# Huber loss on one core: a block of 32x2560 numbers taken apart from the tiles, with a full second tile and narrower end tiles

## The chip, the cores and the metric

The kernel runs on one core of one Trainium2 chip. The metric is the time on the device in microseconds (us), taken from the median of several runs. Three runs of the kernel before gave 1866.98, 1867.10 and 1867.79 us. The engines that matter here are the vector engine (DVE), the scalar engine (ACT), the queue that issues transfers (SyncE, SP) and the core's 16 DMA engines, which carry out every transfer that SP issues.

## The reference

Two arrays of 8192x8192 float32 go in and one comes out, so 536.87 MB are read from the chip's memory (HBM) and 268.44 MB are written.

```
diff = pred - target
abs_diff = np.abs(diff)
return np.where(abs_diff <= 1.0, 0.5 * diff**2, 1.0 * (abs_diff - 0.5))
```

With a = |pred - target| the kernel computes max(a - 0.5, 0.5 * min(a, 1)^2), which is the same.

## The kernel before

The arrays are taken as flat memory and dealt into tiles. Tile i is a run of 128 rows of `widths[i]` numbers, each row on one partition of the on-chip memory. With W = 14592, GAP = 9408 and R = W - GAP = 5184, the 37 tiles have the widths 9408, 12000, 34 times 14592, and 6752.

One buffer, `mem`, of 128 rows by 3W + GAP = 53184 numbers holds everything. Tile i's `pred` goes to the place `at_a(i)` and its `target` to `at_b(i)`; even and odd tiles use different places. The two places of `target` (columns 0 and 14592) lie apart. The places of `pred` overlap by 5184 columns for two full tiles: the piece that a tile shares with the next one's `pred` is `covered(i)`.

A tile is worked on in pieces of its columns, and each piece takes five instructions:

- `subtract` (lines 95 and 96): DVE writes pred - target over target, ACT takes the absolute value in place.
- `square` (lines 100 and 103): DVE clips into t, a scratch place inside the tile's used `pred`, ACT squares t with the factor 0.5.
- `combine` (line 107): DVE writes max(a - 0.5, t) over target, which is then the result.

`pieces` (line 111) cuts a part of a tile into pieces of about 5184 columns in the middle, 2592 or less at the start and end, and 1296 or less in the last tile. `work` (line 124) writes out the order by hand, so that DVE has two pieces under way while ACT works on the third. The schedule is manual: every engine runs its instructions in the order in which the program writes them.

`load(i)` (line 74) and `store(i)` (line 82) are issued by SP alone, so all transfers stand in one queue in the program's order. `parts(i)` says in how many column ranges a tile is loaded: halves for the first and for the last two tiles, two unequal parts for the third from the end, otherwise the whole tile at once. The main loop (lines 154 to 160) loads tiles 0 and 1 first. Then, for each tile i, SP issues the store of tile i-1, and, after the first subtraction of tile i (that of the piece that `pred` of the next tile will cover), the loads of tile i+1. The load of `target` of tile i+1 goes where the result of tile i-1 lay, so SP lets it wait until that store has landed.

Of the kernel before, what the change touches and what calls it, by code (L numbers as in the profile page):

```python
# [1 line left out]

# [4 lines left out]


@with_exitstack
def kernel(  # L10
    ctx: ExitStack,
    tc: tile.TileContext,
    pred: bass.AP,
    target: bass.AP,
    out: bass.AP,
):
    nc = tc.nc
    P = 128
    fp32 = mybir.dt.float32
    Alu = mybir.AluOpType  # L20
    Act = mybir.ActivationFunctionType
    SQRT_HALF = 0.70710678118654752

    total = pred.shape[0] * pred.shape[1] // P
    W = 14592
    GAP = 9408
    R = W - GAP
    widths = [GAP, W - R // 2] + [W] * 34
    widths.append(total - sum(widths))
    n = len(widths)  # L30
    starts = [sum(widths[:i]) * P for i in range(n)]

    def block(x, i):
        flat = x.rearrange("r m -> (r m)")
        return flat[starts[i] : starts[i] + P * widths[i]].rearrange("(p m) -> p m", p=P)

    pool = ctx.enter_context(tc.tile_pool(name="memory", bufs=1))
    mem = pool.tile([P, 3 * W + GAP], fp32, name="mem")

    def at_a(i):
        return 3 * W + GAP - widths[i] if i % 2 else 2 * W

    def at_b(i):
        return W if i % 2 else 0

    def covered(i):  # L50

        if i + 1 >= n:
            return (0, 0)
        lo = max(at_a(i), at_a(i + 1))
        hi = min(at_a(i) + widths[i], at_a(i + 1) + widths[i + 1])
        return (lo - at_a(i), hi - at_a(i)) if hi > lo else (0, 0)


    def parts(i):
        w = widths[i]  # L60
        if i == n - 3:
            return [(w - 2 * R, w), (0, w - 2 * R)]
        if i in (0, n - 2, n - 1):
            return halves(w)
        return [(0, w)]

    def halves(w):
        h = w // 32 * 16
        return [(0, h), (h, w)]

    def view(base, lo, hi):
        return mem[:, base + lo : base + hi]

    def load(i):
        order = [(x, part) for part in parts(i) for x in "pt"]
        if i == n - 1:
            order = [(x, part) for x in "pt" for part in parts(i)]
        for x, (lo, hi) in order:
            src, base = (pred, at_a(i)) if x == "p" else (target, at_b(i))
            nc.sync.dma_start(out=view(base, lo, hi), in_=block(src, i)[:, lo:hi])  # L80

    def store(i):
        w = widths[i]
        for lo, hi in halves(w) if i == n - 1 else [(0, w)]:
            nc.sync.dma_start(out=block(out, i)[:, lo:hi], in_=view(at_b(i), lo, hi))

    def split(lo, hi, size):
        k = -((lo - hi) // size)
        edges = [lo + (hi - lo) * j // k // 16 * 16 for j in range(k)] + [hi]
        return list(zip(edges[:-1], edges[1:]))  # L90


    def subtract(i, lo, hi, at):
        a, d = view(at_a(i), lo, hi), view(at_b(i), lo, hi)
        nc.vector.tensor_tensor(out=d, in0=a, in1=d, op=Alu.subtract)  # L95
        nc.scalar.activation(out=d, in_=d, func=Act.Abs)  # L96

    def square(i, lo, hi, at):
        d, t = view(at_b(i), lo, hi), view(at_a(i) + at, 0, hi - lo)
        nc.vector.tensor_scalar(  # L100
            out=t, in0=d, scalar1=-1.0, scalar2=1.0, op0=Alu.max, op1=Alu.min
        )
        nc.scalar.activation(out=t, in_=t, func=Act.Square, scale=SQRT_HALF)  # L103

    def combine(i, lo, hi, at):
        d, t = view(at_b(i), lo, hi), view(at_a(i) + at, 0, hi - lo)
        nc.vector.scalar_tensor_tensor(  # L107
            out=d, in0=d, scalar=-0.5, in1=t, op0=Alu.add, op1=Alu.max
        )

    def pieces(i, lo, hi):


        c0, c1 = covered(i)
        c0, c1 = max(lo, c0), min(hi, c1)
        if c1 <= c0:
            k = -((lo - hi) // (R // 2 if i < n - 1 else R // 4))
            return [], [(i, x, y, x) for x, y in split(lo, hi, -((lo - hi) // k))]
        x, y = (lo, c0) if c0 > lo else (c1, hi)
        m = max(c1 - c0, (y - x) // 32 * 16)  # L120
        rest = [(x, x + m), (x + m, y)] if y > x + m else [(x, y)]
        return [(i, c0, c1, x)], [(i, x, y, x) for x, y in rest]

    def work(i, then):

        todo, held = [], []
        for part in parts(i):
            first, rest = pieces(i, *part)
            todo += first + rest
            held += first  # L130
        mid, end = [], []
        if held:
            subtract(*todo.pop(0))
        then()
        while todo or mid or end or held:
            if todo:
                piece = todo.pop(0)
                subtract(*piece)
                mid.append(piece)
                if len(mid) < 2 and todo:  # L140
                    continue
            if mid:
                piece = mid.pop(0)
                square(*piece)
                end.append(piece)
                if len(end) < 2 and (todo or mid):
                    continue
            combine(*end.pop(0))
            mid += held
            held = []  # L150

    ctx.enter_context(tc.manual_schedule())

    load(0)
    load(1)
    for i in range(n):
        if i > 0:
            store(i - 1)
        work(i, lambda: load(i + 1) if 0 < i < n - 1 else None)
    store(n - 1)  # L160


# [1 line left out]
_INS = ['pred', 'target']  # L164
_OUTS = [((8192, 8192), 'float32')]


# [23 lines left out]
```

## Time and profile before

| what | value |
|---|---|
| median of 3 runs | 1867.1 us (1866.98 to 1867.79) |
| the profiled execution | 1866.7 us |
| its span, first to last instruction | 1864.9 us |
| DVE busy | 1408.3 us (76%), 357 instructions |
| ACT busy | 912.5 us (49%), 239 instructions |
| DMA queue of SP | 805.31 MB, 99.9% of the 16 engines' span |
| mean DMA rate | 432 GB/s |

The profile tells what each engine did from the first instruction to the last, in one execution. The difference between the span and the execution's own time, 1.8 us, lies around it. The DMA share is the mean of 16 DMA engines: 0.5 can mean that eight of them work and eight have nothing left. The trace also keeps, for every transfer, the times at which its sixteen shares were reported as landed, one for each DMA engine; these are called completion marks below.

### The profile page before, as it was taken

How to read it: one execution, taken by the hardware profiler on the slowest of the kernel's cores; microseconds unless marked ns; L12 is line 12 of the kernel's file. 1: busy time of each engine (PE TensorE's matmuls, PEld its weight loads, DVE VectorE, ACT ScalarE, POOL GpSimd, SP SyncE). 2: the span in 40 equal slices, each digit the busy share in tenths (PEclk: the TensorE clock that was granted, in tenths of full speed). 3: DMA queues.
4: the chain of work that ended last, by engine and by line, in shares of the span. 5: the costliest groups of instructions: out<-in, count | busy, mean ns of one | idle time of the engine just before them, and what ended most of it. 6: DMA issues, size and time to landing. Idle time of an engine off the chain costs nothing.

```text
span 1864.9 us, 960 instructions
## 1 busy us (share of the span) xinstructions
DVE 1408.3 (76%) x357; ACT 912.5 (49%) x239; POOL 0.2 (0%) x4
## 2 busy tenths in 40 slices
DVE  5677777777788777777778877777777887777986
ACT  3455444444555545444455554544445555454554
POOL 0000000000000000000000000000000000000000
DMA  9999999999999999999999999999999999999999
GB/s 421 418 436 431 436 431 432 437 427 436 438 428 434 439 428 435 438 429 433 438 428 436 438 428 435 438 428 436 438 427 437 436 429 437 435 429 436 428 437 393
DMA packets 17287, 805.37 MB, mean 432 GB/s; under 512 B 1920, under 2 KB 1920, under 8 KB 1920
## 3 DMA queue, kind: packets, MB, share of 16 engines
q1 hardware_dynamic: 17280, 805.31, 99.9%
q14 instruction: 7, 0.06, 0.0%
HBM read 536.87 MB, written 268.44 MB: 432 GB/s over the span
## 4 chain that ended last, share of the span: by engine, by line
DMA 56%; DVE 26%; ACT 13%; issue 4%; another core or an unknown queue 1%; SPq 0%; DVEq 0%
DMA mem<-in_target_dram 32%; DMA out_dram<-mem 24%; DVE mem L107 11%; DVE mem L95 11%; ACT mem L103 8%; ACT mem L96 4%; DVE mem L100 3%; SPq L80 0%; DVEq L95 0%
## 5 line engine op out<-in xcount | busy, mean ns | idle before, releaser
L96 ACT ACTIVATE mem<-mem 128x5184 f32<-128x5184 f32 (+8 forms) x119 | 459.2, 3874 | 756.3 <-DVE mem L95 756.2
L95 DVE TENSOR_TENSOR mem<-mem 128x5184 f32<-128x5184 f32 (+8 forms) x119 | 558.5, 4743 | 336.2 <-DMA mem<-in_target_dram 336.2
L107 DVE SCALAR_TENSOR_TENSOR mem<-mem 128x5184 f32<-128x5184 f32 (+8 forms) x119 | 564.4, 4745 | 74.5 <-ACT mem L103 70.6
L103 ACT ACTIVATE mem<-mem 128x5184 f32<-128x5184 f32 (+8 forms) x119 | 456.7, 3864 | 169.2 <-DVE mem L100 169.2
L100 DVE TENSOR_SCALAR mem<-mem 128x5184 f32<-128x5184 f32 (+8 forms) x119 | 292.0, 2453 | 34.9 <-ACT mem L96 29.9
L96 ACT ACT_TABLE_LOAD x1 | 1.3, 1283 | 14.6 <-DMA mem<-in_target_dram 14.6
L175 POOL MEMSET const-bfloat16-1.0<- 128x1 bf16 x1 | 0.1, 103 | 0.0
L175 POOL MEMSET const-uint8-127<- 128x1 uint8 x1 | 0.1, 102 | 0.0
L175 POOL MEMSET const-float32-0.0<- 128x1 f32 x1 | 0.1, 100 | 0.2 <-issue 0.2
L175 POOL MEMSET const-float32-1.0<- 128x1 f32 x1 | 0.1, 99 | 0.0
## 6 DMA issues: line engine op xcount, KB each, us to landing
out_dram<-mem SPq DMA_DIRECT2D x34, 7296.0 KB, 26.5
mem<-in_pred_dram SPq DMA_DIRECT2D x32, 7296.0 KB, 28.7
mem<-in_target_dram SPq DMA_DIRECT2D x32, 7296.0 KB, 34.4
mem<-in_pred_dram SPq DMA_DIRECT2D x2, 3648.0 KB, 27.6
mem<-in_target_dram SPq DMA_DIRECT2D x2, 3648.0 KB, 25.5
mem<-in_pred_dram SPq DMA_DIRECT2D x1, 6000.0 KB, 36.8
mem<-in_target_dram SPq DMA_DIRECT2D x1, 6000.0 KB, 51.5
out_dram<-mem SPq DMA_DIRECT2D x1, 6000.0 KB, 24.6
```

What stands on the lines that cost most here:

```text
L95: nc.vector.tensor_tensor(out=d, in0=a, in1=d, op=Alu.subtract)
L96: nc.scalar.activation(out=d, in_=d, func=Act.Abs)
L100: nc.vector.tensor_scalar(out=t, in0=d, scalar1=-1.0, scalar2=1.0, op0=Alu.max, op1=Alu.min)
L103: nc.scalar.activation(out=t, in_=t, func=Act.Square, scale=SQRT_HALF)
L107: nc.vector.scalar_tensor_tensor(out=d, in0=d, scalar=-0.5, in1=t, op0=Alu.add, op1=Alu.max)
L175: nc = _bacc.Bacc("TRN2", target_bir_lowering=False, num_devices=1)
```

## The change

A block of 32 rows by 2560 numbers (81920 numbers, 327,680 bytes, at the end of the arrays) is no longer part of any tile. It has a place of its own in the buffer, behind tile 0's `target`, and is computed with tile 0, as one piece that goes through the same five instructions on 32 partitions. It is loaded (two transfers) between the first and the second half of tile 0, and stored (one transfer) after tile 0's instructions. In HBM the block is addressed as eight groups of four rows of 2560 numbers.

Tile 1 becomes full (12000 to 14592 columns) and is loaded in two parts, 10368 and 4224 columns. The second part is issued by SP only after the block's store. The last but one tile goes from 14592 to 13056 columns, the last from 6752 to 5056; there are still 37 tiles. The rest of the diff passes views where it passed a tile's number and columns.

```diff
-    widths = [GAP, W - R // 2] + [W] * 34
-    widths.append(total - sum(widths))
+    C = 2560
+    widths = [GAP] + [W] * 34 + [13056]
+    widths.append(total - C // 4 - sum(widths))
...
     def parts(i):
         w = widths[i]
+        if i == 1:
+            return [(0, 2 * R), (2 * R, w)]
...
+    def lone(x):
+        flat = x.rearrange("r m -> (r m)")
+        return flat[P * sum(widths) :].rearrange("(r g m) -> g r m", g=8, r=4)
+
+    def lone_at(k):
+        return mem[0:32, GAP + k * C : GAP + (k + 1) * C]
+
     ctx.enter_context(tc.manual_schedule())
 
-    load(0)
-    load(1)
-    for i in range(n):
-        if i > 0:
-            store(i - 1)
-        work(i, lambda: load(i + 1) if 0 < i < n - 1 else None)
+    first, second = parts(0)
+    load(0, [first])
+    nc.sync.dma_start(out=lone_at(0), in_=lone(pred))
+    nc.sync.dma_start(out=lone_at(1), in_=lone(target))
+    load(0, [second])
+    load(1, parts(1)[:1])
+    alone = [(lone_at(1), lone_at(0), lone_at(0))]
+    work(pieces(0, *first)[1] + alone + pieces(0, *second)[1])
+    nc.sync.dma_start(out=lone(out), in_=lone_at(1))
+    load(1, parts(1)[1:])
+    for i in range(1, n):
+        store(i - 1)
+        work_on(i, lambda: load(i + 1) if i < n - 1 else None)
     store(n - 1)
```

## The prediction

> **What bounds the kernel now.** I read the page's busy shares and DMA queue first, then the DMA share and rate by stages, then the queue's waits and the order of time at both ends, and last the completion marks. From the page:
>
> ```profile
> span 1864.9 us, 960 instructions
> DVE 1408.3 (76%) x357; ACT 912.5 (49%) x239; POOL 0.2 (0%) x4
> q1 hardware_dynamic: 17280, 805.31, 99.9%
> ```
>
> The 16 DMA engines are busy 99.9% of the span, DVE 76%. The table of stages (time range, length, DVE, ACT, POOL busy, PEclk, DMA share, GB/s) shows no hole in the stream:
>
> ```profile
> 0.00:4.00 4.00, 0.00 (x0) 0.00 (x0) 0.20 (x4) 1.00 0.60 198
> 4.00:50.00 46.00, 25.50 (x12) 18.26 (x9) 0.00 (x0) 1.00 1.02 440
> 50.00:56.00 6.00, 0.73 (x1) 0.00 (x0) 0.00 (x0) 1.00 0.94 328
> ...
> 98.00:150.00 52.00, 39.16 (x9) 25.27 (x6) 0.00 (x0) 1.00 1.00 428
> 150.00:410.00 260.00, 195.80 (x45) 126.33 (x30) 0.00 (x0) 1.00 1.00 433
> 410.00:1700.00 1290.00, 979.01 (x225) 631.63 (x150) 0.00 (x0) 1.00 1.00 434
> ```
>
> At 434 GB/s the 805.31 MB take 1855.5 us; the span is 9.4 us longer. The change leaves the bytes alone, so it can only touch these 9.4 us or open a hole. The last stretch shows one part of them:
>
> ```profile
> 1859.00:1860.00 1.00, 0.00 (x0) 0.00 (x0) 0.00 (x0) 1.00 1.02 432
> ...
> 1860.50:1861.00 0.50, 0.00 (x0) 0.00 (x0) 0.00 (x0) 1.00 0.58 243
> ...
> 1861.50:1862.00 0.50, 0.00 (x0) 0.00 (x0) 0.00 (x0) 1.00 0.57 243
> 1862.00:1862.50 0.50, 0.00 (x0) 0.00 (x0) 0.00 (x0) 1.00 0.38 162
> ...
> 1863.00:1863.50 0.50, 0.00 (x0) 0.00 (x0) 0.00 (x0) 1.00 0.13 54
> ```
>
> The engines do not end together: share 0.57 is nine of sixteen, 0.13 two. The completion marks of the last store agree: 1860.67 for the first engine, seven within 0.68 us, the eighth at 2.02, the last at 1864.11, which is 3.43 later. The mean lies 1.78 before the last: that much a perfect balance would save. The spread was 0.88 at the first landing (8.10 to 8.97), 2.72 at 272 us, 3.19 at 427 us, and stayed. It grew mostly in the last packets of `target` loads, just before the stream turns to a store: by the last mark 1.14 us were lost at the first turn (all engines, the 328 GB/s above), then 0.80 near 150, 0.47 near 203 and 255, 0.20 and 0.28 near 358 and 410.
>
> The order of time and the queue's waits show how far SP is ahead (start, duration, what; then who waited for whom: us in total, times, longest):
>
> ```profile
> 44.92 0.35 SPq L85 DMA_DIRECT2D out_dram<-mem  x1
> ...
> 55.27 12.80 DVE L95 TENSOR_TENSOR mem<-mem 128x2592 f32<-128x2592 f32 x3 [10.38 <-DMA mem<-in_target_dram]
> ...
> 1789.08 5.29 DVE L95 TENSOR_TENSOR mem<-mem 128x2432 f32<-128x2432 f32 x2
> ...
> 1831.85 22.48 SPq L85 DMA_DIRECT2D out_dram<-mem  x3
> ...
> SPq L85 <- DVE mem L107: 880.9, 38, 27.7
> ...
> SPq L80 <- DMA out_dram<-mem: 415.9, 35, 32.2
> ```
>
> SP waits nearly all the time, yet each transfer is issued before the one ahead of it is done: the first store at 44.92, when tile 1's target lands at 55.18; in the steady part 9.2 us ahead (issued 1072.59, target landed 1081.84).
>
> **The change part by part.** *Bytes per engine.* A block transfer is 327,680 bytes. One engine moves 434/16 = 27.1 GB/s. Spread over sixteen, three such transfers are 61,440 bytes or 2.26 us an engine, as now. Over eight they are 122,880 bytes or 4.53 us on these and nothing on the rest: +2.26 on eight engines, -2.26 on eight. Every transfer of before has 128 rows and sixteen marks, so no row shows which; the ends are 0 and 2.26. I take eight, because a leading dimension of eight cannot be dealt evenly to sixteen.
>
> *How much of it reaches the end.* What counts is how far ahead of the last engine those eight were. Ends: 0, if the last one is among them, and 1.41 (3.43 - 2.02), if they are the eight earliest. The trailing order is there at the first landing and grows where an engine already trails, so eight engines served first would be the leading ones: I take 1.41. Term: +2.26 - 1.41 = +0.85, upper end +2.26.
>
> *Turns from load to store.* The block's store is one more turn. Beside it the eight engines trail the others by 3.0 us after the block's loads and 4.5 after its store, more than the 3.2 at which the late stalls ceased. So the turns after the first may cost nothing: a gain of up to 0.80 + 0.47 + 0.47 + 0.20 + 0.28 = 2.2. Or the trailing eight are hit as trailing engines were: a loss of up to the first turn's 1.1. I take 0, between the two.
>
> *Five more transfers* (125 for 120). A short load cost 0.05 us over its bytes in the marks of the last four loads: +0.2.
>
> *Compute beside tile 0.* The block adds, by the 2592-column rows (DVE 2.86, 1.51 and 2.85, ACT 2.36 and 2.36), about 7.1 us on DVE and 4.7 on ACT; 32 partitions are in no row, so the ends are 0 and that. Tile 0's second target landed at 25.72; it now lands up to 3.0 later, 28.7 on the eight engines. From there DVE runs 2.6 + 1.5 + 2.6 + 2.6 + 1.4 + 2.8 = 13.5 to the block's last instruction: about 42.3. Only then does SP issue the block's store, and behind it tile 1's second part. The stream has tile 1's first part until 28.7 + 2 x 12.3 = 53.3 on the eight engines and 50.3 on the rest (the 10368-column target load near the end took 12.3 by its marks, 1731.33 to 1743.62). So that wait is covered by 8.0 us and more. Tile 0 ends at about 42.3 + 1.4 + 5.2 = 48.9 (before 44.9); its store has the second part's 10 us as further cover. Tile 1's load of the next `pred` waits for its first subtraction, 53.3 + 5.6 = 58.9 (before 58.21), with store 0 in the stream until about 75. All this costs 0.
>
> *Steady part.* The tiles from the second on are as before; tile 1 starts on its first part 10 us before it is whole, so the first margin grows. With eight engines 4.5 us ahead, the 9.2 us margin leaves these 4.7, against 1.0 from an issue to its first packet (0.73 to 1.74): cost 0.
>
> *Tail.* DVE took 1789.08 to 1831.83, 42.75 us, for 14592 columns: 38.2 for 13056. From the landing of that tile's first half the stream now has two loads of 7.70, a store of 17.21 and four loads of 2.98: 44.5. DVE begins 0.9 after that landing now, and 0.9 + 2 x 0.91 = 2.7 after it then. 44.5 - 2.7 - 38.2 leaves 3.6 (before 7.0) for the store of tile 35. The leading engines may run dry for a microsecond or two, which costs only their lead. The last tile's compute, 19.05 for six pieces, becomes 14.3; its cover is 2.98 + 15.4 + 2.98 = 21.4. Cost 0; if the 3.6 were gone, each us later would be a us at the end.
>
> *Sum*, against the profiled execution's 1866.7 (0.4 under the median of 1867.1): 1866.7 + 0.85 + 0 + 0.2 = **1867.7**.
>
> [...]
>
> **The rivals.** *The last engine is among the eight* (0.18): +2.26 + 0.2, 1869.2. For it: nothing tells which eight; against it, the early order. *The stagger ends the stalls at the turns* (0.22): 1867.7 - 2.2 = 1865.5. For it: they ceased at a spread of 3.2; against it, they also followed trailing engines. *The block goes over all sixteen, so the change does not do what it says* (0.07): 1866.9. *Everything comes back* (0.05, faster): balance 1.78 and all turns 2.2 give 4.0, less the 0.2 of the transfers: 1862.9; it needs both whole. *The sixteen engines are held together at the block* (0.09, the other side): if eight cannot go on to the next transfer while the other eight move the block, each of the three costs all engines 1.51, +2.26, and the two turns around the block's store, at 50 to 56 us, 1.1 each as the first turn did: 1866.7 + 2.26 + 2.2 + 0.2 = 1871.4. It decides once both turns are paid in full. Against it: engines run 3.4 us apart across transfers at a share of 1.00.
>
> **How the numbers follow.** My case has 0.39. Within 0.2% (1863.4 to 1870.8, about what a measurement of this kernel can tell from no change) are my case, the late eight, the ended stalls and the sixteen: 0.86. Faster 0.05, slower 0.09. The range 1865.2 to 1869.6 takes in those four with some tenths and leaves out the two outer ones.
>
> **What would show it.** Right: the DMA share is 1.00 through 50 to 60 us, the block's transfers last about 1.5 us each, the last engines end later and the first ones earlier than now, with a final spread of 4 to 6 us. Wrong: a DMA share well under 1 around the block's store or before the store of tile 35; a final spread under 3 us with an earlier end (the eight were leaders by more than I think, or the stalls are gone).

## The result, and the profile after

The changed kernel takes 1872.05 us (median; 1870.64 to 1874.13), the kernel before 1867.17 us on the same chip (1866.47 to 1867.88). The ratio is 1.0027, with a 95% interval of 1.0018 to 1.0035: slower by 3.4 to 6.5 us, where 1867.7 and a range up to 1869.6 had been forecast.

The profiled execution took 1870.64 us, the shortest of its runs, 3.94 above the profiled execution of before. Its page:

```profile
span 1868.9 us, 977 instructions
...
DVE 1413.5 (76%) x360; ACT 916.0 (49%) x241; POOL 0.2 (0%) x4
...
q1 hardware_dynamic: 17688, 805.31, 99.8%
q14 instruction: 8, 0.07, 0.0%
```

The bytes are the same, and the DMA engines are still busy 99.8% of the span. (The last line, the queue that the page calls instruction, will matter below; its packets of 8192 bytes are called fetches here.) The table of stages of the changed kernel (time range, length, busy time of DVE, ACT and POOL, PEclk, DMA share, GB/s):

```profile
4.00:50.00 46.00, 32.36 (x15) 22.71 (x11) 0.00 (x0) 1.00 1.01 432
50.00:56.00 6.00, 1.63 (x1) 0.00 (x0) 0.00 (x0) 1.00 0.96 365
98.00:150.00 52.00, 36.68 (x10) 25.26 (x6) 0.00 (x0) 1.00 1.00 432
150.00:410.00 260.00, 196.95 (x46) 126.32 (x30) 0.00 (x0) 1.00 1.00 434
410.00:1700.00 1290.00, 975.88 (x225) 631.27 (x150) 0.00 (x0) 1.00 1.00 434
1700.00:1820.00 120.00, 100.20 (x35) 63.06 (x23) 0.00 (x0) 1.00 1.00 427
1820.00:1858.00 38.00, 33.55 (x22) 21.71 (x15) 0.00 (x0) 1.00 0.98 414
```

The last two stages of before, in the same columns:

```profile
1700.00:1820.00 120.00, 105.76 (x34) 70.40 (x23) 0.00 (x0) 1.00 1.00 432
1820.00:1858.00 38.00, 30.87 (x24) 19.61 (x15) 0.00 (x0) 1.00 0.99 427
```

There is no stage in which all engines stand still. In the two long stages the rates are those of before. They are lower in the first row (432 against 440) and in the tail (427 against 432, 414 against 427), and higher at the first turn (365 against 328). So the 3.9 us are to be looked for in how the work is dealt to the sixteen engines, and in the tail. The last microseconds of the changed kernel show it, in the same columns:

```profile
1862.00:1863.00 1.00, 0.00 (x0) 0.00 (x0) 0.00 (x0) 1.00 0.65 273
1863.00:1864.00 1.00, 0.00 (x0) 0.00 (x0) 0.00 (x0) 1.00 0.29 121
1864.00:1865.00 1.00, 0.00 (x0) 0.00 (x0) 0.00 (x0) 1.00 0.21 91
1865.00:1866.00 1.00, 0.00 (x0) 0.00 (x0) 0.00 (x0) 1.00 0.24 101
1866.00:1867.00 1.00, 0.00 (x0) 0.00 (x0) 0.00 (x0) 1.00 0.12 51
```

A share near 0.2 for three microseconds is three or four engines of sixteen still at work. The completion marks of the last store run from 1862.51 to 1867.47, a spread of 4.96 (before 1860.67 to 1864.11, spread 3.43). So the first engine ends 1.84 later than before and the last one 3.36 later. Another 0.64 lies between the last mark and the end of the span (1.43 against 0.79).

The marks also tell how the block is carried. Each of its transfers has eight completion marks of data, every other transfer sixteen. Its packets of 10,240 bytes take 385 ns, four on each engine, and the last marks step by about 1.5 us: 14.77 for the load ahead of it, 16.30 and 17.83 for the block's two. The first marks step in the same way, 13.86, 15.38 and 16.92. So the eight engines that carry the block hold both the first and the last of the sixteen. The spread of one transfer's marks, which was 0.92 before the block, is 3.86 after its loads and 5.5 after its store, in two groups of eight: 0 to 0.8 and 4.7 to 5.5.

Where the last engine loses time over its bytes can be added up from the last marks: the step from one last mark to the next, less the bytes of that transfer on one engine at 434/16 = 27.125 GB/s. The level of these sums moves with the third digit of the rate (at 27.10 they are 3.43 and 4.39); their difference does not. In us, by stage, from the first landing on:

```
                 to 150  block  150-430  430-1700  1700-1830  end    sum    last mark
before            1.65     -      2.25     0.60       0.39    0.25   5.14   1864.11
after             1.12    0.06    1.11     1.69       0.81    1.31   6.10   1867.47
```

The bytes alone give the last engine 2.26 more. Its losses fell by 1.6 in the first 430 us and rose by 2.6 behind that. Another 0.14 was there at the first landing (9.11 against 8.97); together these make the 3.36.

Compute followed its plan. From the order of time of the changed kernel (start, duration, engine, line and operation):

```profile
39.37 2.81 DVE L107 SCALAR_TENSOR_TENSOR mem<-mem 32x2560 f32<-32x2560 f32 x1
...
42.20 0.71 SPq L178 DMA_DIRECT2D out_dram<-mem  x1
42.96 0.44 SPq L83 DMA_DIRECT2D mem<-in_pred_dram  x1
...
48.54 0.35 SPq L88 DMA_DIRECT2D out_dram<-mem  x1
60.01 0.33 SPq L83 DMA_DIRECT2D mem<-in_pred_dram  x1
```

The block's last instruction ends at 42.2, SP issues the block's store then (line 178) and tile 1's second part right behind it, and all of that lies ahead of a queue that is still full.

### The profile page after: what moved, and what is told of

It reads as the page before. It is cut to its first block, busy times and chain, and to the rows that moved or that the text cites. A ratio compares the mean times of both kernels' runs of the same rounds, so it can differ in the third digit from the quotient of the medians.

```text
span 1868.9 us, 977 instructions
## 1 busy us (share of the span) xinstructions
DVE 1413.5 (76%) x360; ACT 916.0 (49%) x241; POOL 0.2 (0%) x4
## 3 DMA queue, kind: packets, MB, share of 16 engines
q1 hardware_dynamic: 17688, 805.31, 99.8%
## 4 chain that ended last, share of the span: by engine, by line
DMA 58%; DVE 25%; ACT 12%; issue 3%; SPq 0%; DVEq 0%
DMA mem<-in_target_dram 33%; DMA out_dram<-mem 25%; DVE mem L107 11%; DVE mem L97 11%; ACT mem L104 8%; ACT mem L98 4%; DVE mem L101 3%; SPq L83 0%; SPq L172 0%; SPq L173 0%; DVEq L97 0%
## 5 line engine op out<-in xcount | busy, mean ns | idle before, releaser
L98 ACT ACTIVATE mem<-mem 128x5184 f32<-128x5184 f32 (+7 forms) x120 | 461.0, 3857 | 754.9 <-DVE mem L97 754.7
L97 DVE TENSOR_TENSOR mem<-mem 128x5184 f32<-128x5184 f32 (+7 forms) x120 | 560.8, 4721 | 337.3 <-DMA mem<-in_target_dram 337.3
L104 ACT ACTIVATE mem<-mem 128x5184 f32<-128x5184 f32 (+8 forms) x120 | 458.6, 3846 | 169.4 <-DVE mem L101 169.4
```

## The experiments

Two theories stood at first. The skew theory: the time is lost because eight engines carry the whole block, and the last engine is one of them. The tile theory: the time is lost through the tiles' new sizes, the extra turn and the order of the transfers. Later variants of the skew theory differ in what comes on top of the eight engines' share of the bytes. Every time below is a median beside the kernel before on the same chip (1867.17 to 1867.25); a ratio has its 95% interval. The last two runs are single executions.

**The block over sixteen engines.** The changed kernel, with the block addressed as 32 rows in place of eight groups of four:

```diff
-        return flat[P * sum(widths) :].rearrange("(r g m) -> g r m", g=8, r=4)
+        return flat[P * sum(widths) :].rearrange("(q m) -> q m", q=32)
```

> The changed kernel, only the block is addressed in HBM as 32 rows instead of eight groups of four, so that its three transfers should go over all sixteen DMA engines. Skew theory (eight engines carry 2.26 us more than their share and all of it reaches the end): 1866.5 to 1868.0, as before, with a final spread near 3.4 us. Tile theory (the narrower end tiles, with 3.6 us of cover for the store of tile 35 instead of 7.0, cost the time): 1871 to 1873, as the changed kernel.

Measured: 1869.18 us (1868.48 to 1871.70), ratio 1.0013 (1.0004 to 1.0022). That is 2.9 less than the changed kernel, but 2.0 more than before, which was no theory's number. The block's transfers now have sixteen marks and the spread at the end is 3.77. But the packets of 10,240 bytes take 589 and 800 ns in the median of its two loads where they took 385, and a load of the block takes 1.6 us (last marks 16.64 and 18.27). The stage of the block's loads, in the changed kernel and then in this one (columns as above):

```profile
14.00:19.00 5.00, 4.13 (x2) 2.77 (x2) 0.00 (x0) 1.00 1.05 448
```

```profile
14.00:19.00 5.00, 3.89 (x2) 2.53 (x2) 0.00 (x0) 1.00 1.01 279
```

All sixteen engines are busy in both, but with 32 rows they move 279 GB/s. So spread over sixteen engines the block's two loads still cost twice their bytes' time, only now on every engine: 0.87 us each over their bytes, most of the 2.0. The block's store does not: its packets take 385 to 395 ns, and it moves the last mark by 0.77 us, which is its bytes' time. Uneven engines were not the whole story, and what slows the loads does not slow the store.

**The block with the tiles of before.** The changed kernel with tiles 1, 35 and 36 as they were (12000 columns in one part, 14592, and 6112 to take the block out):

```diff
-    widths = [GAP] + [W] * 34 + [13056]
+    widths = [GAP, W - R // 2] + [W] * 34
...
-        if i == 1:
-            return [(0, 2 * R), (2 * R, w)]
...
-    load(1, parts(1)[:1])
+    load(1)
...
-    load(1, parts(1)[1:])
```

> The block on eight engines alone: tile 1 keeps 12000 columns in one part, the tiles 35 and 36 are 14592 and 6112 columns wide. Skew theory: 1869.4 (2.26 us over before) to 1872, with the leading engines 5 us and more ahead. Tile theory: 1866.5 to 1868.0.

Measured: 1871.16 us (1868.64 to 1877.57), ratio 1.0021 (1.0013 to 1.0030). The loss is there without the new tile sizes and without the wait in front of tile 1's second part, so these two do not make it. The extra turn is still in this kernel; the run over 128 partitions below answers for it.

**The transfers alone, in eight groups and as 32 rows.** The kernel before, with three spare loads of the block's form behind tile 0's loads. Nothing uses what they bring.

```diff
+    for k, at in enumerate((GAP, GAP + 2560, 2 * W + GAP)):
+        spare = pred.rearrange("r m -> (r m)")[k * 81920 : (k + 1) * 81920].rearrange("(r g m) -> g r m", g=8, r=4)
+        nc.sync.dma_start(out=mem[0:32, at : at + 2560], in_=spare)
```

> The kernel before with three spare loads of 32x2560 numbers (into unused columns, not computed on) between tile 0 and tile 1, each in eight groups of four rows. It moves 0.98 MB more than needed. Skew theory: these are 4.53 us on eight engines and nothing on the rest, so 1871.7 if the last engine is always among the eight, 1870.3 if the eight lead by 1.4 us as I forecast. If only the bytes count and not the engines that move them: 1869.4.

The same with 32 rows:

```diff
-        spare = (...).rearrange("(r g m) -> g r m", g=8, r=4)
+        spare = (...).rearrange("(q m) -> q m", q=32)
```

> The same three spare loads, addressed as 32 rows, so over sixteen engines: 2.26 us on each. Every theory: 1869.4. The difference to the spare loads on eight engines is the price of the skew alone: 2.26 us by the skew theory, 0 if only bytes count.

Measured: eight groups 1874.15 us (1871.39 to 1876.51), ratio 1.0034 (1.0022 to 1.0045); 32 rows 1871.65 (1871.00 to 1873.03), 1.0024 (1.0015 to 1.0034). Both missed every expectation, by 2.4 and 2.2 us. The second is +4.5, which is twice the 2.26 of the bytes. The last engine spends no longer on the three loads in eight groups, 4.6 us by the last marks (25.67 to 30.28), than as 32 rows, 4.8 us (26.29 to 31.06). So the 2.5 us between the two times are what uneven engines cost on top. The stage of the spare loads, eight groups first, then 32 rows:

```profile
25.00:28.00 3.00, 2.24 (x1) 0.00 (x0) 0.00 (x0) 1.00 1.03 439
```

```profile
25.00:28.00 3.00, 1.62 (x1) 0.00 (x0) 0.00 (x0) 1.00 1.07 225
```

(Where eight groups move, the other eight engines go on with tile 1, so the rate stays full.) With 32 rows the rate is half, 225 GB/s, with every engine busy; the packets take 793 ns in the median.

**The block over 128 partitions.** The changed kernel, with the same numbers laid as 128 rows of 640:

```diff
-        return flat[P * sum(widths) :].rearrange("(r g m) -> g r m", g=8, r=4)
+        return flat[P * sum(widths) :].rearrange("(p m) -> p m", p=P)
...
-        return mem[0:32, GAP + k * C : GAP + (k + 1) * C]
+        return mem[:, GAP + k * (C // 4) : GAP + (k + 1) * (C // 4)]
```

> The changed kernel with the block laid over all 128 partitions, 128 rows of 640 numbers, nothing else changed. Theory A (two costs: a transfer to 32 partitions takes about 1.6 us whether eight or sixteen engines carry it, and eight engines that carry more reach the end later): 1866.5 to 1867.8, as before, since neither is left. Theory B (the block's store as one more turn between loads, or the tile widths, cost some of the time): 1868.5 to 1870.

Measured: 1867.31 us (1866.67 to 1868.35), ratio 1.0000 (0.9991 to 1.0009). With only the block's shape changed, the whole loss is gone. The same stage of the block's loads, then the page's first line and rows of the last microseconds:

```profile
14.00:19.00 5.00, 4.37 (x2) 3.01 (x2) 0.00 (x0) 1.00 1.08 452
```

```profile
span 1865.3 us, 977 instructions
```

```profile
1860.00:1861.00 1.00, 0.00 (x0) 0.00 (x0) 0.00 (x0) 1.00 0.51 212
...
1862.00:1863.00 1.00, 0.00 (x0) 0.00 (x0) 0.00 (x0) 1.00 0.21 91
1863.00:1864.00 1.00, 0.00 (x0) 0.00 (x0) 0.00 (x0) 1.00 0.05 20
```

Tile 1's two parts, the extra turn, the narrower end and the order are all still in this kernel, and together they cost nothing that can be measured. (The block's five instructions are shorter too, and its store is issued at 37.52; but in the changed kernel they were not waited for either.) The end of its span also lies 1.39 behind its last mark (1863.91), so that part of the changed kernel's longer span is also there in a kernel that is no slower.

**One spare transfer in eight groups.** As the spare loads above, with the loop over `(GAP,)`:

> The kernel before with one spare load of 32x2560 numbers in eight groups instead of three. If the price is the load on the eight engines, in proportion: 1867.2 + 1.51 = 1868.7, up to 1869.5 with a third of the further 2.4 us that three of them cost. If a stagger of 1.5 us between two halves of the engines saves the stalls at the turns: 1866.5 or less.

Measured: 1869.93 us (1868.73 to 1871.69), ratio 1.0015 (1.0006 to 1.0024). One such load is 1.51 us on its eight engines; 2.7 were lost, more than the 1869.5 that was expected at most. A small stagger gains nothing either: it costs its bytes and 1.2 more.

**Spare loads over 128 and over 64 partitions.** The same three spare loads as 128 rows of 640, and as 64 rows of 1280 on partitions 0 to 63:

```diff
-        spare = (...).rearrange("(r g m) -> g r m", g=8, r=4)
-        nc.sync.dma_start(out=mem[0:32, at : at + 2560], in_=spare)
+        spare = (...).rearrange("(q m) -> q m", q=128)
+        nc.sync.dma_start(out=mem[0:128, at : at + 640], in_=spare)
```

> The kernel before with three spare loads of the same 327,680 bytes, but as 128 rows of 640 numbers. Theory A (32 partitions take data at half the rate of 128): 0.75 us each, 1867.2 + 2.3 = 1869.5, against 1871.65 with 32 rows over sixteen engines. If any three further transfers at this place cost 4.5 us: 1871.7.

> The same three spare loads as 64 rows of 1280 numbers, on partitions 0 to 63. [...]

Measured: 128 partitions 1869.51 us (1868.63 to 1870.23), ratio 1.0012 (1.0004 to 1.0021), which is the 2.3 us of the bytes and nothing else; 64 partitions 1871.69 (1871.29 to 1872.50), 1.0025 (1.0015 to 1.0035), which is the price of 32 rows. The stage of the spare loads, 128 partitions first, then 64 (a packet is counted whole where it starts, so the first rate is over 434):

```profile
25.00:28.00 3.00, 2.15 (x1) 0.00 (x0) 0.00 (x0) 1.00 1.38 570
```

```profile
25.00:28.00 3.00, 1.51 (x1) 0.00 (x0) 0.00 (x0) 1.00 1.02 227
```

A packet of 5,120 bytes takes 396 ns in the median on the 64 partitions. So loads to 0 to 63 are as slow as loads to 0 to 31 (227 and 225 GB/s, where the steady part of the kernel before has 434 with 128 partitions): twice as many partitions did not make them faster. Why the rate is halved was not shown, and no run loaded other partitions than these. The store of 32 rows above shows no such halving (385 to 395 ns a packet).

**A wider tail.** The changed kernel with tile 35 at 14592 columns and so a last tile of 3520:

```diff
-    widths = [GAP] + [W] * 34 + [13056]
+    widths = [GAP] + [W] * 35
```

> The changed kernel with tile 35 at its old 14592 columns, so that the last tile has 3520. Its halves last 8.6 us instead of 7.7, so the engines that lead by 7 us find the next transfer in time. If the 0.53 and 1.01 us that the last engine lost in the tail come from the leaders running dry there: about 1 us less than the changed kernel's 1872.05, 1870.5 to 1871.3. If they come from the eight loaded engines alone: 1871.8 to 1872.3.

Measured: 1873.94 us (1873.47 to 1874.86), ratio 1.0036 (1.0024 to 1.0049). This run does not answer its question, because it opened a hole. The loads of the short last tile landed at 1847.46, but tile 35 was not computed until SP issued its store at 1848.14. The order of time and the stages of this kernel:

```profile
1848.14 0.34 SPq L88 DMA_DIRECT2D out_dram<-mem  x1
```

```profile
1846.00:1848.00 2.00, 2.00 (x1) 0.00 (x0) 0.00 (x0) 1.00 0.05 21
1848.00:1851.00 3.00, 2.98 (x5) 1.82 (x3) 0.00 (x0) 1.00 0.73 311
```

All sixteen engines ran dry, and the last of them lost 2.79 us there. So a lack of cover at the tail is paid for. The turn ahead of the hole is not touched by it: the leading engines had run dry for 1.2 us before it, and the last one lost 0.02 at it (last mark 1821.77), where it lost 0.53 in the changed kernel. That is one execution; whether the tail's stalls go away with a wider tile 35 stays open.

**Half a block.** The changed kernel with `C = 1280` in place of 2560, so a share of 1.13 us more on eight engines:

> The changed kernel with a block of half the size (C = 1280, the last tile 320 columns wider), eight groups. If the further cost grows with the share moved: 1867.2 + 1.13 + 1.3 = 1869.6. If the share alone counts: 1868.3. If the further cost is there in full as soon as the eight engines have no lead (the instruction fetches then fall on the last engines): 1870.3 to 1871.

Measured: 1871.17 us (1868.85 to 1877.31), ratio 1.0023 (1.0014 to 1.0032), a little over the highest expectation. The share of the bytes alone would give 1868.3. What comes on top is here 2.8 us, so it does not shrink with the block (2.6 with the whole one). It is not the same everywhere: 1.7 with the tiles of before, 1.2 with one spare load.

**Both again.** The changed kernel and the one with half a block, each profiled once more, because the first profiles were of their fastest executions:

> The changed kernel as it is, profiled once more, because its first profile (1870.64) was the fastest of its fourteen runs and the median is 1872.05. If the execution is slower than 1871.5, its completion marks tell where the further time goes. Stalls theory: in losses of 0.2 to 1.4 us at single turns from load to store and in instruction fetches, both on the eight engines that carry the block, at other places than in the first profile. If a hole in the stream appears instead, in a stage where the DMA share falls for all engines, the schedule is short of cover.

> The half-size block profiled once more: its first profile, 1868.85, was the fastest of its eleven runs (median 1871.17, up to 1877.31). Stalls theory: as for the changed kernel, losses at single turns, more of them than in the first profile. If the eight engines' share alone counted, no execution should lie above 1868.3 by more than 1 us.

Measured: 1872.42 and 1870.14 us, the kernel before 1867.5. The first lies next to its kernel's median, so its losses are the ones to explain. The second lies above the 1869.3 that would be the limit if the share alone counted. The last microseconds of the first (columns as above):

```profile
1864.00:1866.00 2.00, 0.00 (x0) 0.00 (x0) 0.00 (x0) 1.00 0.35 147
1866.00:1868.00 2.00, 0.00 (x0) 0.00 (x0) 0.00 (x0) 1.00 0.17 71
```

The losses of the last engine over its bytes in all profiles, by the same sum as above. In the upper group every transfer is dealt evenly; in the lower group eight engines carry more. The column of the block takes in the spare loads:

```
                                to 150  block  150-430  430-1700  1700-1830  end    last mark
even      before                 1.65     -      2.25     0.60       0.39    0.25   1864.11
          block over 128         0.99    0.16    2.01     1.21       0.34    0.26   1863.91
          block as 32 rows       0.97    1.76    2.60     0.71       0.37    0.24   1865.55
          three spare over 128   1.26    0.20    1.73     0.60       0.41    0.28   1865.72
          three spare, 32 rows   1.03    2.50    2.08     1.53       0.34    0.29   1869.02
          three spare, 64 rows   0.99    2.52    2.58     0.92       0.36    0.29   1868.99
uneven    after                  1.12    0.06    1.11     1.69       0.81    1.31   1867.47
          after again            0.82    0.02    2.32     2.39       0.61    1.79   1869.25
          half block             1.44    0.04    0.76     1.95       0.36    1.20   1865.67
          half block again       1.24   -0.04    1.74     2.06       0.72    1.07   1866.97
          tiles of before        0.97   -0.13    2.92     2.09       0.34    0.29   1867.92
          three spare, eight     1.24    0.08    1.48     2.91       0.64    1.44   1871.23
          one spare, eight       1.42    0.00    2.20     1.32       0.39    0.25   1866.23
          wider tail (hole)      1.27   -0.15    3.31     2.67       0.41    3.03   1871.69
```

From 430 us to the end the even kernels lose 1.2 to 2.2 us, the uneven ones without the hole 2.0 to 5.0. Single losses of 0.1 us and more show of what kind they are. In the changed kernel they come at turns (the end of a target's load, just before a store), here by the last mark at which they show: 54.28 (0.75), 318.41 (0.28), 370.27 (0.19), 422.40 (0.48), 1815.65 (0.53), 1845.94 (1.01). Three more show in transfers during which an instruction fetch came: 905.10 (0.56), 1129.08 (0.14), 1577.42 (0.65). In its second profile the transfers with a fetch lost 0.44, 0.81 and 0.81 (233.76, 906.60, 1578.93), two turns 0.88 each (163.54, 216.10), and the tail's two turns 0.31 and 1.56. In the kernel before the last engine lost nothing at a fetch and nothing at a turn of the tail. The other profiles say the same of the fetches: single losses in such transfers add up to 0.8 to 2.2 us in the seven profiles in which eight engines carry a block or three spare loads, and to nothing in all six even ones. With one spare load none is over 0.11, so what its median lost over its bytes is not explained by its profile (1868.80, near its fastest). At turns the even kernels lose 2.4 to 3.6 in all and the uneven ones 2.5 to 4.6, so the turns differ less.

The fetches are the q14 packets of the page, 8192 bytes each, seven to eight in 1870 us. In the trace of a kernel in eight groups the marks of a transfer during which a fetch came are late by some 0.5 to 1.1 us in sum. In the eight profiles of kernels with transfers in eight groups there are 48 of them before the tail. Each time the delay shows among the eight marks that trail, which are those of the engines with the block (the later group of eight above): one of these moves by 0.24 to 0.82 us over its bytes, while no mark of the leading eight moves by more than 0.08. In the changed kernel the six start at 220.0, 286.8, 676.9, 893.1, 1115.0 and 1565.4 us and last 309 to 318 ns each; taken in order of time, the mark that moves most is a trailing one each time, by 0.50 to 0.62.

So the time is accounted for in this way. From the kernel with the block over 128 partitions to the changed kernel the medians differ by 4.7 us. Of these 2.26 are the bytes that sit on eight engines in place of sixteen. The other 2.5 come with the uneven engines. In the two profiles of the changed kernel the marks show 1.1 and 3.0 us of further losses. At fetches they lose 1.3 and 2.1, where the kernel over 128 partitions loses nothing, and at turns 0.2 and 1.6 more than it. The reading is that these delays fall on engines that are last by construction, so that no slack is left to take them up. That uneven engines cost more than their bytes is shown by the runs; that the fetches make most of it is read from the marks, and no run moved the block to the other eight engines or took the fetches away.

## Why the prediction was wrong

- *Bytes per engine* was right: the block's transfers have eight marks each, 385 ns for 10,240 bytes and about 1.5 us a transfer. That it would be eight was the author's choice between two ends, since no trace of before showed it; addressed as 32 rows the same block had sixteen marks.
- *How much of it reaches the end* is the step that failed. It took the eight engines to be leaders with 1.41 us in hand. But when the block came, the last engine was among the eight (marks 14.77 to 16.30), and so was the first. Over its bytes the last of them loses 6.10 us by its marks (7.94 in the profile next to the median), the last engine of before 5.14. There was no lead to spend; the 2.26 came through whole, with some 2.5 on top. In all 48 fetches the mark that moved was also one of the trailing eight, by 0.24 to 0.82 us. The early order could say nothing of this: in the trace of before the first fetch inside the stream comes at 260.7 us.
- *Turns from load to store* was mis-sized at 0. The gain that the stagger rival saw is there in part: the last engine's losses to 430 us fell from 3.90 to 2.29, and to 3.16 in the profile near the median. But this is outweighed by what was lost in transfers with a fetch and at the turns of the tail.
- *Tail* was mis-sized. The leaders did run dry, near 1785 and 1834 us (for 1.5 and 1.0 by the first marks), where SP issues the next loads only when the last engine has landed the store. The step said that this costs only their lead. But the last engine then lost 0.53 and 1.01 us at the tail's turns (0.31 and 1.56 in the second profile), where before it lost none. That engines which had run dry and come back in step make the trailing ones stall is a guess. The tiles of before with the block had leaders that lost 0.8 and 0.9 us of their lead at such places, and its last engine lost only 0.29 at the end. The first tail turn of the wider tail speaks against the guess too, but that run opened a hole before it could decide.
- *Five more transfers*, *Compute beside tile 0* and *Steady part* were right: the kernel with the block over 128 partitions has them all (its block with shorter instructions) and takes the time of before. The block's store was issued at 42.20 (forecast 42.3), tile 0's at 48.54 (48.9), the next load of `pred` at 60.01 (58.9).
- *What would show it*: the share stayed near 1 around the block (0.96 in 50 to 56 us, before 0.94), the transfers took 1.5 us, and the spread of 4.96 was in the forecast 4 to 6. But the first engines end later than before, not earlier.
- Of the rivals, *the last engine is among the eight* (1869.2) had the right mechanism and lacked the 2.5 us on top. *The block over all sixteen* (1866.9) would not have been free, had it been so: the experiment that did it took 1869.18. *Sixteen engines held together* has a time that is near (1871.4), but not its mechanism: while eight engines carry the block, the others go on, and the stage of its loads moves 448 GB/s.

What stays open: why loads to partitions 0 to 31 and 0 to 63 go at half the rate, why the tail's turns stall in the uneven kernels, why one spare load costs 1.2 over its bytes, and why their unprofiled runs scatter further than their profiles tell (up to 1877.3 with half a block, 1877.6 with the tiles of before). No version was found that beats the kernel before; the block over 128 partitions equals it.

## What to carry to other kernels

Where the DMA engines bound a kernel, the price of a change is read from the engine that ends last: count the bytes of each transfer per engine, and take an uneven share as paid in full, with something on top (here 2.26 us and about 2.5), unless marks of those very engines show that they are ahead. A small block is laid over all 128 partitions, even if its rows become short: loaded to partitions 0 to 31 (by eight engines or by sixteen) or to 0 to 63 (by sixteen) it took twice the time of its bytes over all sixteen engines, 1.5 to 1.6 us in place of 0.75, while as 128 rows it lost only 0.07 us over its bytes.

## What the runs showed of the hardware

- Loads to partitions 0 to 31 and to 0 to 63 moved 225 and 227 GB/s with all sixteen engines busy (shares 1.07 and 1.02), against 434 in the steady part with 128 partitions. Why was not shown. A load of 327,680 bytes to 32 partitions took about as long on eight engines (1.5 us) as on sixteen (1.6 us). The one store from 32 partitions over sixteen engines was not slowed: 385 to 395 ns a packet where the loads took 589 and 800, and 0.77 us in all.
- Packets of 2,560 bytes over 128 partitions cost little over their bytes: 102 ns each, 0.07 us a load over its bytes by the marks, and three spare loads made the kernel 2.3 us longer.
- In transfers during which a packet of the q14 queue came (8192 bytes, 309 to 318 ns in the changed kernel), marks were late by 0.5 to 1.1 us in sum. In the kernels with transfers in eight groups (48 such packets in eight profiles) the mark that moved, by 0.24 to 0.82 us, was always one of the eight that trail after the block.
- The block's instructions over 32 partitions took as long as those over 128 with about as many columns: DVE 2.81, 1.48 and 2.81 us and ACT 2.32 for 32x2560 in the changed kernel, where DVE had 2.86, 1.51 and 2.85 and ACT 2.36 for 128x2592 in the kernel before. The forecast took the latter.
